# Turning the softmax numerators of the odd heads by DMA instead of on TensorE, in a decoder trunk on one core

## The chip, the core and the metric

One NeuronCore of a Trainium2 chip. Its engines are called PE (TensorE, matrix products), ACT (ScalarE), DVE (VectorE), POOL (GpSimd) and SP (SyncE, which here only issues DMAs). The metric is the device time of one execution in microseconds, lower is better; the time of a kernel is the median of its runs.

## The reference

Two layers over 512 tokens of width 1024, all in float32: a gated short convolution with an MLP, then sparse attention with an MLP, with RMS norms around them. The change is in the attention. There are 16 heads of 64 in 4 groups; the four heads of a group share keys and values. Cut to what matters:

```python
def one_block(qb):                                   # 128 queries
    ...
    logit_c = einsum('bqghd,bngd->bqghn', qt, k_cmp) + bias_c      # 31 compressed blocks
    p_c = softmax(where(valid_c, logit_c, NEG_INF)) * has_any
    o_c = einsum('bqghn,bngd->bqghd', p_c, v_cmp)
    ...
    logit_s = einsum('bqghd,bqgkd->bqghk', qt, ks) + bias_s        # selected blocks
    o_s = einsum('bqghk,bqgkd->bqghd', softmax(where(valid_s, logit_s, NEG_INF)), vs)
    logit_w = einsum('bqghd,bkgd->bqghk', qt, kw) + bias_w[None]   # window of 512
    o_w = einsum('bqghk,bkgd->bqghd', softmax(where(valid_w, logit_w, NEG_INF)), vw)
    return gt[..., 0:1] * o_c + gt[..., 1:2] * o_s + gt[..., 2:3] * o_w
```

The bias is a learned table over 32 buckets of distance, one column per head. With 512 tokens there are 8 blocks to select from and all of them are chosen, so the selected branch and the window branch are both full causal attention, with keys and values of their own.

## The kernel before

**Numbers.** Products are made in fp16 with each operand split into a high and a low half: ACT writes the high half (a scaled copy), DVE the rest (`scaled value - high half`). A product then takes three matmuls (`mm3`: high x high, high x low, low x high). Weights arrive as float32 in pieces, are split by `convert_piece` (L189, L190) and used.

**The attention stage.** Work is cut into items. `Full(g, qb, br, h)` is one head `h` of group `g`, one block `qb` of 128 queries, one branch `br` (selected or window), over `nk = 128 (qb + 1)` keys, that is `nb = qb + 1` blocks of 128. There are 128 of them, 32 per group. `Cmp(g, qb)` is the compressed branch of a group's four heads, 16 items. The order is `full(0) + full(1) + cmps(0) + cmps(1) + full(2) + cmps(2) + cmps(3) + full(3)`. Each item goes through stages at fixed distances behind the front of the list (`lead`):

- `st0`: two products of the queries with the high and the low half of the keys (L878, L879) into a bank "b"; one DVE operation (L883) adds the bias and takes the extreme of each row, from PSUM into a tile `at_s`; ACT takes the exponential and its sum (L886) into `at_p`, float32, one row per query.
- `st1`, two items later: the numerators must stand with the keys on the partitions before they can be multiplied with the values. PE transposes `at_p` block by block in fp32 (L892) into a bank "c"; ACT writes the high half `at_ph` from there (L895).
- `st2`, three items later: DVE writes the low half `at_pl` (L898).
- `st3`, four items later: three products with the values for each block (L910 to L912), into a bank "d" that collects both branches and four heads; after the last head DVE applies the gates and denominators (L921) and POOL adds up.
- `st4`, six items later: `finish` transposes the sum and splits it for the output projection.

Between the stages of the items, a generator `background` puts pieces of projections, 1.7 per item for the first 64 items and 0.9 after: raw keys of the compressed branch (`raw`), the MLP that compresses them (`phi`), the queries of groups 1 to 3 (`queries`), the first half of the output projection. The tile framework places the semaphores and, where an engine's next instruction would wait, may let a later one of the text go first, so the order on an engine is close to the text and not the same.

**The bias.** The row of biases of a head by distance lies in DRAM (`ext_d`). `load_T(g)` reads it as a Hankel matrix, row p shifted by p, for the four heads of a group in one DMA of ACT's queue (L585) into a tile `T` of 128 x 4 x 528 float32, two of them; a small copy `Tc` (L589) holds every 16th column for the compressed branch.

**Shared tiles.** `at_s` (three buffers of 128 x 512 float32) is also taken by `scaled` (L607), whose result ACT and POOL split into queries (L702, L703), and by `raw`, which writes the re-ordered raw keys there (L721) and splits them into `kr_hl` (one buffer, L351, L353); six DMAs on SP then copy that into `big` (L727 to L729). `phi_hd` (L776) is a tile of `phi` that is used once.

Of the kernel before, what the change touches and what calls it, by code (L numbers as in the profile page):

```python
# [29 lines left out]
SP = 1024.0  # L30
# [18 lines left out]
def body(ctx, tc, x, rel_bias, norm_mix, norm_mlp, mlp_w1, mlp_w2, a_w_in, a_conv_w, a_w_out,  # L49
# [512 lines left out]
    with pool("attn") as ap:  # L562
# [17 lines left out]
            DVE.memset(hmask[32 * h:32 * h + 32, h:h + 1], SV / (SR * SW))  # L580
        ot = None

        def load_T(g):
            t = ap.tile([128, 4, TW], F32, name="T", bufs=2)
            nc.scalar.dma_start(t, bass.AP(tensor=ext_d.tensor, offset=ext_d.offset + 4 * g * EXT,  # L585
                                           ap=[[1, 128], [EXT, 4], [1, TW]]))
            TG[g] = t
            c = ap.tile([128, 4, 32], F32, name="Tc", bufs=4)
            DVE.tensor_copy(c, t[:, :, 0:512:16])  # L589
            TC[g] = c  # L590

        load_T(0)
        rbk = rbq = rtok = None
# [9 lines left out]
            DVE.tensor_scalar(rtok[:, 1], r, 1.0 / (SW * SX), None, op0=OP.mult)  # L603

        def scaled(ps, rb):
            t = ftile("at_s", 3)
            DVE.tensor_tensor(t, ps, rb, op=OP.mult)  # L607
            return t

# [100 lines left out]
        def raw(which):  # L710
            po = yield from gated_pair(xkv)
            kr = ap.tile([128, 2, 8, S], F16, name="big", bufs=1)
            DVE.memset(kr[:, :, 4], 0.0)
            DVE.memset(kr[64:128, :, 0:4, S - 1:S], 0.0)
            for half in range(2):
                at = slice(half, S, 64)
                split_to(kr[:, 0, 4, at], kr[:, 1, 4, at], pet[:, which, 8 * half:8 * half + 8], SK)
            for m in range(2):
                t = ftile("at_s", 3)
                by_stride = lambda a: a.rearrange("p (b r) -> p r b", r=16)  # L720
                DVE.tensor_tensor(t.rearrange("p (r b) -> p r b", r=16), by_stride(po[m]), by_stride(rbk),  # L721
                                  op=OP.mult)
                hl = ap.tile([128, 2, S], F16, name="kr_hl", bufs=1)
                split_to(hl[:, 0], hl[:, 1], t)
                for s in range(2):
                    g, r = 2 * m + s, slice(64 * s, 64 * s + 64)
                    nc.sync.dma_start(kr[0:64, :, g, :], hl[r])  # L727
                    nc.sync.dma_start(kr[64:128, :, g, 0:S - 32], hl[r, :, 32:S])
                    nc.sync.dma_start(kr[64:128, :, g, S - 32:S - 1], hl[r, :, 1:32])  # L729
                yield  # L730
            KRs[which] = kr
# [3 lines left out]
        def phi(which):  # L735
            kr = KRs[which]
            ph = [bank("a"), bank("a")]
            for quarter in range(4):
                w = next_piece()
                cv = ahead_fine()  # L740
                for c in range(4):
                    cc = 4 * quarter + c
                    at = 64 * (cc % 8) + cc // 8
                    rhs = [kr[:, hl, 0:5, at:at + 31] for hl in range(2)]
                    for m in range(2):
                        o = ph[m][:, 0:155].rearrange("p (g j) -> p g j", g=5)
                        mm3(o, [u[:, c, m * 128:(m + 1) * 128] for u in w], rhs, cc == 0, cc == 15)
                        next(cv, None)
                    yield
                drain(cv)  # L750
            hs = ap.tile([128, 2, 2, G, 32], F16, name="phi_h", bufs=1)
            DVE.memset(hs[:, :, :, :, 31:32], 0.0)
            for m in range(2):
                bcol = ap.tile([128, 1], F32, name="phi_b", bufs=2)
                ACT.activation(bcol, ph[m][:, 124:125], AF.Copy, scale=1.0 / (SW * SK))
                t = ap.tile([128, G, 31], F32, name="phi_t", bufs=2)
                ACT.activation(t, ph[m][:, 0:124].rearrange("p (g j) -> p g j", g=4), AF.Silu,
                               bias=bcol, scale=1.0 / (SW * SK))
                split_to(hs[:, m, 0, :, 0:31], hs[:, m, 1, :, 0:31], t, SR)
            for _ in range(4):  # L760
                yield
            w = next_piece()
            if which == 0:
                pk = bank("e")
                w2 = [ap.tile([128, 2, 2, 64], F16, name=f"phi_w2{i}") for i in range(2)]
                for i in range(2):
                    for d in range(2):
                        DVE.tensor_copy(w2[i][:, :, d], w[i])
                for m in range(2):
                    mm3(pk[:, 0:128], [u[:, m].rearrange("p a b -> p (a b)") for u in w2],  # L770
                        [hs[:, m, i].rearrange("p g j -> p (g j)") for i in range(2)], m == 0, m == 1)
                split_to(KC[:, 0], KC[:, 1], pk[:, 0:128].rearrange("p (g j) -> p g j", g=4), SK / (SR * SW))
                yield
            else:
                pv = bank("e")
                hd = ap.tile([128, 2, 2, G, 4, 32], F16, name="phi_hd")  # L776
                for m in range(2):
                    for i in range(2):
                        DVE.tensor_copy(hd[:, m, i], hs[:, m, i][:, :, None, :].to_broadcast([128, G, 4, 32]))
                for g in range(4):  # L780
                    o = pv[:, g * 64:(g + 1) * 64]
                    for m in range(2):
                        lh = [hd[:, m, i, g].rearrange("p h n -> p (h n)") for i in range(2)]
                        PE.matmul(o, lh[0], w[0][:, m], start=m == 0, stop=False)
                        PE.matmul(o, lh[0], w[1][:, m], start=False, stop=False)
                        PE.matmul(o, lh[1], w[0][:, m], start=False, stop=m == 1)
                for g in range(4):
                    t = ap.tile([128, 4, 64], F32, name="vc_t", bufs=1)
                    DVE.tensor_tensor(t, pv[:, None, g * 64:(g + 1) * 64].to_broadcast([128, 4, 64]),
                                      hmask[:, :, None].to_broadcast([128, 4, 64]), op=OP.mult)  # L790
                    split_to(VC[:, 0, g], VC[:, 1, g], t)
                yield
            drain(ahead())
# [68 lines left out]
        class Full(Item):  # L862
            def __init__(self, g, qb, br, h):
                self.g, self.qb, self.br, self.h = g, qb, br, h
                self.nb = qb + 1
                self.nk = 128 * self.nb

            def need(self):
                return [f"q{self.g}"]

            def st0(self):
                g, qb, br, h, nk = self.g, self.qb, self.br, self.h, self.nk
                if (g, qb) not in obank:
# [3 lines left out]
                q = Qs[g][:, h, qb * 128:(qb + 1) * 128]  # L877
                PE.matmul(s[:, :nk], q, KD[:, br, 0, g, :nk], start=True, stop=False)  # L878
                PE.matmul(s[:, :nk], q, KD[:, br, 1, g, :nk], start=False, stop=True)  # L879
                lg = ftile("at_s", 3)  # L880
                mn = ap.tile([128, 1], F32, name="at_m", bufs=3)
                lo = 128 * qb + PAD
                DVE.tensor_tensor_reduce(lg[:, :nk], s[:, :nk], TG[g][:, h, lo:lo - nk:-1], -1.0 / SL, 3e38,  # L883
                                         OP.add, OP.min, mn)
                self.p = ftile("at_p", 3)
                ACT.activation(self.p[:, :nk], lg[:, :nk], AF.Exp, bias=mn, scale=-1.0,  # L886
                               accum_out=l[:, br * 4 + h:br * 4 + h + 1])

            def st1(self):
                pt = bank("c")  # L890
                for b in range(self.nb):
                    PE.transpose(pt[:, b * 128:(b + 1) * 128], self.p[:, b * 128:(b + 1) * 128], ident)  # L892
                self.pt = [ap.tile([128, S], F16, name=n, bufs=3) for n in ("at_ph", "at_pl")]
                self.ps = pt[:, :self.nk]
                ACT.activation(self.pt[0][:, :self.nk], self.ps, AF.Copy, scale=SP)  # L895

            def st2(self):
                DVE.scalar_tensor_tensor(self.pt[1][:, :self.nk], self.ps, SP, self.pt[0][:, :self.nk],  # L898
                                         op0=OP.mult, op1=OP.subtract)

# [126 lines left out]
                if next(bg, "end") in ("wait", "end"):  # L1027
                    return

        lead = {1: 2, 2: 3, 3: 4, 4: 6}  # L1030
        credit = 0.0
        for i in range(len(items) + 6):
            if i < len(items):
                it = items[i]
                for k in it.need():
                    while k not in done:
                        if next(bg, "end") == "end":
                            raise RuntimeError(k)
                if isinstance(it, Full):
                    if it.g not in TG:  # L1040
                        load_T(it.g)
                    if (it.qb, it.br, it.h) == (2, 0, 0) and it.g < 3 and it.g + 1 not in TG:
                        load_T(it.g + 1)
                elif it.g not in TC:
                    load_T(it.g)
                it.st0()
            credit += 1.7 if i < 64 else 0.9
            while credit >= 1.0:
# [126 lines left out]
```

## Time and profile before

| | |
|---|---|
| median of 3 runs | 1161.62 us (1160.56 to 1163.6) |
| the profiled execution | 1161.23 us, span 1159.4 us |
| mean granted TensorE clock | 0.990 |
| PE busy | 1109.1 us, 96% |
| DVE busy | 839.8 us, 72% |
| ACT busy | 579.0 us, 50% |
| POOL busy | 146.9 us, 13% |
| attention stage | about 562 to 797 us of the span |

The span runs from the first to the last instruction; the execution's own time has 1.8 us more around it. Busy times count the work of an engine, not its waits. Matmuls are pipelined, so that the busy time of PE, the length of each matmul is more than PE would need at its peak rate. A line such as L330 belongs to the helper `mm3` and has many callers; the tile names tell them apart.

### The profile page before, as it was taken

Reading aid. Unit: us, or ns where it says so; the run is one execution under the profiler, and the core shown is the slowest. Engines: PE = TensorE matmul, PEld = TensorE weight load, DVE = VectorE, ACT = ScalarE, POOL = GpSimd, SP = SyncE. Lnnn points to the kernel's source line nnn. Section 1 sums busy time; section 2 is a strip of 40 time slices with the busy share of each in tenths; the row PEclk is TensorE's granted clock in tenths of the full one; section 3 lists DMA queues with packets and bytes.
Section 4 is the critical chain, followed back from the end, with each engine's and each line's share of the span. In section 5 each row is a group of like instructions: output and inputs, shape, how many; then the busy total and the mean of one; then the engine's idle time right before and its main releaser. Section 6 shows DMA issues by size and latency. Waiting matters only on the chain.

```text
span 1159.4 us, 20318 instructions
## 1 busy us (share of the span) xinstructions
PE 1109.1 (96%) x7947; PEld 694.8 (60%) x7947; DVE 839.8 (72%) x1613; ACT 579.0 (50%) x965; POOL 146.9 (13%) x195
## 2 busy tenths in 40 slices
PE   8999999999999999999899899999999999999886
PEld 3444444447884458858466665665444787446775
DVE  5655458765897557997587898996995698654884
ACT  6322235345343444457579778675544434343442
POOL 0000000422000220000120033111122100123000
PEclk9999999999999999999999999999999999999988
DMA  6432335433433333224233431111733333330321
GB/s 191 126 108 92 109 106 171 121 94 92 128 103 110 98 109 110 92 66 129 89 94 105 119 94 37 38 38 37 212 98 109 110 110 110 109 91 1 94 70 73
DMA packets 147892, 115.76 MB, mean 100 GB/s; under 512 B 8645, under 2 KB 144037, under 8 KB 147797
## 3 DMA queue, kind: packets, MB, share of 16 engines
q1 hardware_dynamic: 145216, 109.47, 31.1%
q10 hardware_dynamic: 2420, 4.48, 1.3%
q8 instruction: 62, 1.02, 0.4%
q0 software_dynamic: 160, 0.52, 0.1%
q14 instruction: 34, 0.27, 0.1%
HBM read 110.22 MB, written 2.14 MB: 97 GB/s over the span
## 4 chain that ended last, share of the span: by engine, by line
PE 51%; DVE 19%; ACT 10%; issue 7%; POOL 6%; DMA 4%; SPq 1%; DVEq 0%; ACTq 0%; POOLq 0%
POOL ml_z L465 6%; PE a L330 5%; PE a L331 5%; PE a L332 4%; DMA wst<-mlp_w_dram 4%; DVE wlo L179 4%; PE b L330 3%; PE b L331 3%; ACT rh L466 3%; PE b L332 3%; PE c L331 3%; PE c L332 3%; PE c L330 3%; DVE wlo L190 3%; DVE wst L176 2%
## 5 line engine op out<-in xcount | busy, mean ns | idle before, releaser
L189 ACT ACTIVATE whi<-wst 128x1024 f16<-128x1024 f32 (+3 forms) x169 | 141.7, 864 | 131.9 <-PE b L331 39.7
L190 DVE SCALAR_TENSOR_TENSOR wlo<-wst,whi 128x1024 f16<-128x1024 f32 (+3 forms) x169 | 167.9, 1001 | 42.1 <-ACT whi L189 42.1
L465 POOL TENSOR_TENSOR ml_z<-ml_z 128x256 f32<-128x256 f32 x128 | 101.1, 810 | 611.2 <-ACT ml_z L463 405.7
L178 ACT ACTIVATE whi<-wst 128x1792 f16<-128x1792 f32 x64 | 106.8, 1691 | 131.4 <-DVE wst L176 93.5
L332 PEld LDWEIGHTS <-wlo 128*128 128x128 f16 x1024 | 100.6, 98 | 109.2 <-issue 2.1
L330 PEld LDWEIGHTS <-whi 128*128 128x128 f16 x1024 | 100.9, 99 | 108.4 <-issue 1.8
L331 PEld LDWEIGHTS <-whi 128*128 128x128 f16 x1024 | 100.6, 98 | 106.7 <-issue 3.8
L467 DVE TENSOR_TENSOR rl<-ml_z,rh 128x1792 f16<-128x1792 f32 x32 | 64.8, 2025 | 135.8 <-ACT rh L466 135.8
L179 DVE SCALAR_TENSOR_TENSOR wlo<-wst,whi 128x1792 f16<-128x1792 f32 x64 | 128.8, 2018 | 6.3 <-ACT whi L178 5.9
L176 DVE TENSOR_TENSOR wst<-wst 128x256 f32<-128x256 f32 x256 | 104.7, 451 | 22.5 <-DMA wst<-mlp_w_dram 21.5
L466 ACT ACTIVATE rh<-ml_z 128x1792 f16<-128x1792 f32 x32 | 54.3, 1697 | 103.3 <-POOL ml_z L465 103.3
L512 PEld LDWEIGHTS <-whi 128*128 128x128 f16 x896 | 88.0, 98 | 18.7 <-ACT ml_t L1087 7.2
L514 PEld LDWEIGHTS <-wlo 128*128 128x128 f16 x896 | 88.0, 98 | 16.7 <-issue 5.0
L513 PEld LDWEIGHTS <-whi 128*128 128x128 f16 x896 | 88.1, 98 | 11.6 <-issue 0.6
L463 ACT ACTIVATE ml_z<-ml_t 128x1024 f32<-128x1024 f32 x32 | 33.8, 1057 | 93.9 <-DVE ml_t L461 93.9
L332 PE MATMUL b<-xsh,wlo 128*128 128x512 f16 x208 | 78.8, 379 | 0.0
L331 PE MATMUL b<-xsl,whi 128*128 128x512 f16 x208 | 78.8, 379 | 0.0
L330 PE MATMUL b<-xsh,whi 128*128 128x512 f16 x208 | 78.7, 379 | 0.0
L886 ACT ACTIVATE at_p<-at_s,at_m 128x128 f32<-128x128 f32 (+3 forms) x128 | 71.3, 557 | 13.7 <-DVE at_m L883 13.3
L512 PE MATMUL a<-rh,whi 128*128 128x256 f16 x256 | 70.5, 275 | 7.0 <-DVE xsh L1089 7.0
L513 PE MATMUL a<-rl,whi 128*128 128x256 f16 x256 | 70.5, 275 | 4.5 <-DVE rl L467 4.5
L883 DVE CUSTOM_DVE_ANT_0 at_s<-b,T 128x128 f32<-128x128 f32 (+3 forms) x128 | 60.9, 479 | 17.0 <-PE b L879 6.6
(292 smaller groups left out, 2761.1 us busy)
## 6 DMA issues: line engine op xcount, KB each, us to landing
wst<-mlp_w_dram SPq DMA_DIRECT2D x256, 256.0 KB, 3.3
wst<-a_w_in_dram SPq DMA_DIRECT2D x24, 512.0 KB, 3.7
wst<-w_kv_dram SPq DMA_DIRECT2D x12, 512.0 KB, 3.5
T<-ext_d ACTq DMA_DIRECT2D x4, 1056.0 KB, 6.6
wst<-a_w_out_dram SPq DMA_DIRECT2D x8, 512.0 KB, 3.4
wst<-b_w_qg_dram SPq DMA_DIRECT2D x8, 512.0 KB, 4.2
wst<-b_w_o_dram SPq DMA_DIRECT2D x8, 512.0 KB, 3.3
xt<-x_dram SPq DMA_DIRECT2D x8, 256.0 KB, 3.7
```

The lines of the kernel that those rows point to most:

```text
L176: DVE.tensor_tensor(b[:, :, o], b[:, :, x], b[:, :, y], op=e)
L178: ACT.activation(hi, b[:, :, 1:], AF.Copy, scale=sc)
L179: DVE.scalar_tensor_tensor(lo, b[:, :, 1:], sc, hi, op0=OP.mult, op1=OP.subtract)
L189: ACT.activation(hi[:, s:e], w, AF.Copy, scale=sc)
L190: DVE.scalar_tensor_tensor(lo[:, s:e], w, sc, hi[:, s:e], op0=OP.mult, op1=OP.subtract)
L330: PE.matmul(ps, w[0], xs[0], start=start, stop=False)
L331: PE.matmul(ps, w[0], xs[1], start=False, stop=False)
L332: PE.matmul(ps, w[1], xs[0], start=False, stop=stop)
L465: POOL.tensor_tensor(z[:, o], z[:, a], z[:, b], op=e)
L466: ACT.activation(rh[0][:, p], z[:, 1:8], AF.Copy)
L512: PE.matmul(acc7[i], wh, xh, start=c == 0 and not other, stop=False, skip_group_check=other)
L513: PE.matmul(acc7[i], wh, xl, start=False, stop=False, skip_group_check=other)
```

## The change

`Full` items with odd `h` are *turned*: `st1` splits `at_p` where it lies, in SBUF, into a tile `at_hl` of 128 x 2nk fp16 (high half, then low half), and one DMA transpose on SP's queue turns all 2nb blocks of 128 x 128 into `at_t`, from which the value products read. Such an item has no `st2`. Even items go through PE as before. For all items the value products come six items behind the front and not four, `finish` eight and not six. Room in SBUF is made: `at_s` has two buffers and not three, `at_ph` and `at_pl` two and not three, the Hankel tiles are held by head (six tiles of one head, loaded one by one, for two tiles of four heads), and `phi_hd` takes the buffer of `kr_hl`, which becomes 128 x 4 x 512.

```diff
-        def load_T(g):
-            t = ap.tile([128, 4, TW], F32, name="T", bufs=2)
-            nc.scalar.dma_start(t, bass.AP(tensor=ext_d.tensor, offset=ext_d.offset + 4 * g * EXT,
-                                           ap=[[1, 128], [EXT, 4], [1, TW]]))
-            TG[g] = t
-            c = ap.tile([128, 4, 32], F32, name="Tc", bufs=4)
-            DVE.tensor_copy(c, t[:, :, 0:512:16])
-            TC[g] = c
+        def load_T(g, heads=range(4)):
+            if g not in TC:
+                TC[g] = ap.tile([128, 4, 32], F32, name="Tc", bufs=4)
+            for h in heads:
+                t = ap.tile([128, TW], F32, name="T", bufs=6)
+                nc.scalar.dma_start(t, bass.AP(tensor=ext_d.tensor, offset=ext_d.offset + (4 * g + h) * EXT,
+                                               ap=[[1, 128], [1, TW]]))
+                TG[g, h] = t
+                DVE.tensor_copy(TC[g][:, h], t[:, 0:512:16])
...
         def scaled(ps, rb):
-            t = ftile("at_s", 3)
+            t = ftile("at_s", 2)
...
-                hl = ap.tile([128, 2, S], F16, name="kr_hl", bufs=1)
+                hl = ap.tile([128, 4, S], F16, name="kr_hl", bufs=1)[:, 0:2]
...
-                hd = ap.tile([128, 2, 2, G, 4, 32], F16, name="phi_hd")
+                hd = ap.tile([128, 4, S], F16, name="kr_hl", bufs=1).rearrange(
+                    "p (m i) (g h n) -> p m i g h n", m=2, g=G, h=4)
...
+                self.turned = h % 2 == 1
...
+            def turn(self):
+                nk, nb = self.nk, self.nb
+                hl = ap.tile([128, 2 * S], F16, name="at_hl", bufs=2)
+                split_to(hl[:, :nk], hl[:, nk:2 * nk], self.p[:, :nk], SP)
+                pt = ap.tile([128, 8, 128], F16, name="at_t", bufs=3)[:, :2 * nb]
+                nc.sync.dma_start_transpose(pt, hl[:, :2 * nk])
+                self.pt = (pt[:, :nb].rearrange("p b q -> p (b q)"), pt[:, nb:].rearrange("p b q -> p (b q)"))
+
             def st1(self):
+                if self.turned:
+                    return self.turn()
...
-                self.pt = [ap.tile([128, S], F16, name=n, bufs=3) for n in ("at_ph", "at_pl")]
+                self.pt = [ap.tile([128, S], F16, name=n, bufs=2) for n in ("at_ph", "at_pl")]
...
             def st2(self):
+                if self.turned:
+                    return
...
-        lead = {1: 2, 2: 3, 3: 4, 4: 6}
+        lead = {1: 2, 2: 3, 3: 6, 4: 8}
...
-                    if it.g not in TG:
-                        load_T(it.g)
-                    if (it.qb, it.br, it.h) == (2, 0, 0) and it.g < 3 and it.g + 1 not in TG:
-                        load_T(it.g + 1)
-                elif it.g not in TC:
-                    load_T(it.g)
+                    if it.g < 3 and (it.qb, it.br, it.h) == (2, 0, 0):
+                        load_T(it.g + 1, (0, 1))
+                    if it.g < 3 and (it.qb, it.br) == (3, 1) and it.h >= 2:
+                        load_T(it.g + 1, (it.h,))
```

More of the change, by code (lines that the diff above doesn't have):

```diff
@@ L718, in raw @@
             for m in range(2):
-                t = ftile("at_s", 3)
+                t = ftile("at_s", 2)
                 by_stride = lambda a: a.rearrange("p (b r) -> p r b", r=16)
@@ L879, in st0 @@
                 PE.matmul(s[:, :nk], q, KD[:, br, 1, g, :nk], start=False, stop=True)
-                lg = ftile("at_s", 3)
+                lg = ftile("at_s", 2)
                 mn = ap.tile([128, 1], F32, name="at_m", bufs=3)
                 lo = 128 * qb + PAD
-                DVE.tensor_tensor_reduce(lg[:, :nk], s[:, :nk], TG[g][:, h, lo:lo - nk:-1], -1.0 / SL, 3e38,
+                DVE.tensor_tensor_reduce(lg[:, :nk], s[:, :nk], TG[g, h][:, lo:lo - nk:-1], -1.0 / SL, 3e38,
                                          OP.add, OP.min, mn)
@@ L1028, in run_bg @@
                     return
-        lead = {1: 2, 2: 3, 3: 4, 4: 6}
+        lead = {1: 2, 2: 3, 3: 6, 4: 8}
         credit = 0.0
-        for i in range(len(items) + 6):
+        for i in range(len(items) + 8):
             if i < len(items):
```

## The prediction

> **What bounds the kernel now.** I read the page first, for the span, then cut the attention stage (first to last work of the `Full` and `Cmp` items, 562 to 797 us; the change touches hardly anything outside it) into stretches, asked for the chain that ended last inside it, and then for its waits.
>
> ```profile
> span 1159.4 us, 20318 instructions
> 562.00:680.00 118.00, 108.71 (x1141) 73.79 (x1140) 93.07 (x280) 94.00 (x256) 13.45 (x14) 0.99 0.35 97
> 680.00:797.00 117.00, 110.63 (x1191) 74.69 (x1189) 108.68 (x391) 86.59 (x263) 27.48 (x40) 1.00 0.15 46
> sum 235.00, PE 219.34 PEld 148.49 DVE 201.76 ACT 180.59 POOL 40.94; mean PE 109.67 PEld 74.24 DVE 100.88 ACT 90.30 POOL 20.47
> ...
> 720.00:780.00 60.00, 58.21 (x641) 40.40 (x641) 58.08 (x208) 43.44 (x135) 8.45 (x14) 1.00 0.15 46
> by line: PE c L892 11.3%; PE a L331 8.9%; PE a L330 8.8%; PE a L332 8.8%; ACT at_p L886 4.7%; PE b L878 4.1%; issue 4.0%; PE b L879 3.9%; PE d L910 3.3%; DVE at_pl L898 3.2%; POOL Q L703 3.1%; DVE at_s L883 2.8%; ACT at_ph L895 2.6%; PE d L
> ```
>
> The columns of the stretches are length, then busy time of PE, weight loads, DVE, ACT and POOL, clock, DMA share, GB/s. In the first half (groups 0 and 1, with much projection work beside them) PE is busy for 108.7 of 118 us and DVE only for 93.1. In the second half DVE is at 108.7 of 117, and from 720 to 780 at 58.1 of 60, 97%. So there are two bounds in turn: PE first, then both with DVE the harder one. On the chain of this stage the largest line is L892, the fp32 transposes of the numerators: 11.3% of 235 us is 26.6 us. That is the work which the change halves.
>
> **What is removed.** A turned item (h odd, 64 of 128) no longer transposes on PE.
>
> ```profile
> L892 PE MATMUL c<-ident,at_p 128*128 128x128 f32 x320 | 57.6, 280 | 6.2 <-DVE at_pl L898 5.5
> L892 PEld LDWEIGHTS c<-ident,at_p 128*128 128x128 f32 x320 | 37.9, 141 | 27.0 <-DVE at_pl L898 9.9 <-issue 4.5 <-ACT at_p L886 2.7
> ```
>
> A group has 2 branches x 4 heads x (1+2+3+4) = 80 blocks; four groups make the 320, and the odd heads own 160. Back to back a transpose follows the one before it at the pace of its fp32 weight load, 141 ns, not at the 280 ns of its busy row, so PE gets 160 x 0.141 = 22.6 us back. How much of that is on the path? Half of L892's share of the chain: 13.3 us. That is the gain I take. Its bounds: 22.6 us if everything that PE gives up is saved, which needs DVE to go from 201.8 to about 212 of 235 without a gap, and nothing if DVE's own queue sets the pace everywhere, as it nearly does between 720 and 780. The turned items also need no bank "c", for which L892 waited on L898 (9.9 us on the weight-load side); this could add a few us and I count it only into the low end of the range.
>
> **What the split costs in its new place.** The two halves of the split stay, one on ACT and one on DVE, but read SBUF.
>
> ```profile
> L895 ACT ACTIVATE at_ph<-c 128x512 f16<-128x512 f32 x32 | 18.7, 586 | 5.6 <-PE c L892 5.6
> L189 ACT ACTIVATE whi<-wst 128x512 f16<-128x512 f32 x41 | 24.7, 623 | 2.7 <-PE a L331 2.7
> L898 DVE SCALAR_TENSOR_TENSOR at_pl<-c,at_ph 128x512 f16<-128x512 f32 x32 | 21.8, 685 | 1.8 <-ACT at_ph L895 1.5
> L190 DVE SCALAR_TENSOR_TENSOR wlo<-wst,whi 128x512 f16<-128x512 f32 x41 | 29.2, 721 | 2.8 <-ACT whi L189 2.8
> ```
>
> L189 and L190 are the same pair of operations from SBUF: 37 ns more on ACT and 36 ns more on DVE. Times 64 that is 2.4 and 2.3 us at the most, into engines that stood idle 54 us (ACT) and 33 us (DVE) in the stage. I take nothing; where DVE is full, the second half, up to 1.2 us would show.
>
> **The DMA transposes.** Each turned item issues one on SP: 128 x 2nk fp16, 64 KB times nb, so 64 to 256 KB, 10.5 MB in all. No transpose by DMA is in this trace. The nearest rows are the copies from SBUF to SBUF of the keys, on the same queue, and above them the loads:
>
> ```profile
> big<-kr_hl SPq DMA_DIRECT2D x8, 128.0 KB, 2.4
> big<-kr_hl SPq DMA_DIRECT2D x8, 7.8 KB, 1.9
> wst<-mlp_w_dram SPq DMA_DIRECT2D x256, 256.0 KB, 3.3
> T<-ext_d ACTq DMA_DIRECT2D x4, 1056.0 KB, 6.6
> L727 SPq DMA_DIRECT2D big<-kr_hl x8: 590/614/702, 580.3 to 648.8; - x8
> ```
>
> Bounds of the landing: 1.9 us (the smallest copy) and 6.6 us (the largest load). I take 2.4 to 3.3 us, by the rows of like size. What it may take: the item is split at two items' distance and its value products are now six behind, four items for split plus landing. The stage is 235 us for 144 items, 1.63 us each; four make 6.5 us. Split, 0.62 + 0.72, and landing, 3.3, make 4.7 us: hidden, with 1.8 us to spare, and the two buffers at_hl (one per two items, so 6.5 us for each) carry it too. Were it late, L910 would stand at the head of PE's queue with the next projections and scores behind it. SP pays some 0.6 us for an issue, 38 us for 64, of 235, beside issues of weights that are as cheap. Weights wait behind a transpose that waits for its DVE half; they are staged pieces ahead, so I take nothing.
>
> On speed the Trainium skill speaks with two voices. "Advanced Engine Details and Errata", X-Bar Transpose (TRN2), has transposing DMAs as fast as ordinary ones; by that the sum above stands. "VectorE: DVE Perf Modes", The three transpose paths, gives 1309 ns for one 128x128 block by DMA against 390 ns on TensorE; 320 blocks one after another would then be an estimated 419 us in a stage of 235. No run before the change shows either.
>
> **What the room for it costs.** SBUF is found by holding less.
>
> *at_s 3 to 2.* This tile takes the logits, the scaled queries and the strided raw keys.
>
> ```profile
> L702 ACT ACTIVATE Q<-at_s x16: 612/627/630, 559.6 to 715.5; 64x512 f16<-64x512 f32 x16
> L703 POOL TENSOR_TENSOR Q<-at_s,Q x16: 1147/1153/1492, 560.3 to 717.4; 64x512 f16<-64x512 f32 x16
> L721 DVE TENSOR_TENSOR at_s<-a,rb x4: 1006/1019/1020, 577.5 to 639.1; 128x512 f32<-128x512 f32 x4
> L351 ACT ACTIVATE kr_hl<-at_s x4: 616/630/631, 578.6 to 645.5; 128x512 f16<-128x512 f32 x4
> DVE at_s L883 <- POOL Q L703: 6.3, 4, 1.8
> DVE at_s L883 <- ACT at_p L886: 3.9, 2, 2.8
> DVE at_pl L898 <- ACT at_ph L895: 7.6, 15, 1.3
> ```
>
> A projection of queries holds two tiles at once, each for two ACT halves and two POOL halves of 1.15 us. With three tiles the logits of DVE already waited there 6.3 us in 4 waits, up to 1.8 us. With two, both can be held, and L883, with all of DVE's later work behind it, waits until the first is free. q1 and q3 fall among `Full` items (q2 among the compressed ones, which don't use at_s): one more longest wait each, 2 x 1.8 = 3.6 us. The second raw tile is written from 639.1 on and read by ACT only at 645.5, after the DMAs of the first; one tile is left for logits meanwhile. I take half the longest wait of DVE on ACT, 0.65 us, for each of two: 1.3 us. Bounds of the whole: nothing if DVE has other work then, 15 us if each of those six tiles costs a 2.5 us stand.
>
> *The keys' DMAs.* L727 to L729 issue six copies of 0.6 us for each raw tile on SP, and one raw phase lies on the chain. Two transposes falling between them, at 0.6 us, make 1.2 us.
>
> *at_ph, at_pl 3 to 2.* Only even items use them now, but an item lives four items, and at its allocation the tile from four items before is still to be read by value products that are next on PE. ACT's high half waits for these, at most 12 products; ACT has the slack (180.6 of 235 us busy), so nothing, and at the worst some 0.3 us x 64 = 19 us. The compressed items keep their buffer counts at the longer distance, so their products come as early as before: nothing.
>
> *Tables by head.* 16 loads of 264 KB in place of 4 of 1056 KB. 12 more issues on ACT, whose row has 366 to 391 ns each, are 4.4 us in ACT's idle 54; the 12 more small copies on DVE, at about 0.2 us, 2 us in its idle 33. Heads 2 and 3 are fetched four items before use, some 6 us: the same cover as above, on the ACT queue. Nothing, and 2 us if DVE has no gap.
>
> ```profile
> L585 ACTq DMA_DIRECT2D T<-ext_d x4: 366/369/391, 507.2 to 678.2; - x4
> L954 DVE TENSOR_TENSOR c_s<-b,Tc x16: 176/218/280, 679.2 to 749.1; 128x32 f32<-128x32 f32 x4, 128x64 f32<-128x64 f32 x4, 128x96 f32<-128x96 f32 x4, 128x128 f32<-128x128 f32 x4
> L886 ACT ACTIVATE at_p<-at_s,at_m x128: 386/570/724, 563.4 to 791.7; 128x128 f32<-128x128 f32 x32, 128x256 f32<-128x256 f32 x32, 128x384 f32<-128x384 f32 x32, 128x512 f32<-128x512 f32 x32
> L910 PE MATMUL d<-VT,at_ph x320: 189/193/203, 569.1 to 796.0; 128*128 128x64 f16 x160
> ```
>
> *The end.* The last item is a turned one. Its exponential ends at 791.7 + 0.7 = 792.4 and its last products came at 796.1, 3.7 us later. Now it is 0.62 + 0.72 + 3.3 + about 0.3 for the products, 4.9 us: 1.2 us more before `finish` and the last output projection.
>
> **The sum.** -13.3 (PE) + 3.6 + 1.3 (at_s) + 1.2 (SP) + 1.2 (end) = -6.0 us. The profiled execution took 1161.23 us (span 1159.4 and 1.8 around it), 0.4 under the median of the three runs, so 1155.2, or 1155.6 on the scale of the median: I say 1155.5.
>
> **Rivals.** *DVE keeps the pace.* PE is relieved, but L883 and L898, which don't shrink, and the stalls on at_s eat the gain. For it: 97% of DVE between 720 and 780. Against it: 25 us of idle DVE before 680. If only the first half's transposes count, half of 13.3, 6.6 us, less the 7.3 us of costs: about 1162, no change.
>
> *Slots in place of PE, slower.* The place is at_s together with at_ph: ACT stands for products, the exponentials come late, and with two tiles the next logits can't start, so DVE stands too. It decides once an item's exponential ends over 1.7 us late (two items, 3.26 us, less the 1.5 us of logits and exponential). At 15 us on at_s and a third of the 19 us on at_ph, against 13.3 of gain and with the other 2.4: 1161 + 15 + 6 + 2 - 13 = 1171.
>
> *A slow turn, slower.* It decides when split and landing pass 6.5 us, a landing of 5.2: then the two at_hl buffers set the pace. At 6.6 us a pair of items takes (1.4 + 6.6) / 2 = 4.0 us in place of 3.26, and 64 pairs add 47 us; the longer half of them only, 24: about 1180 to 1205. Against it: 2.4 us for 128 KB. The serial case of the page on DVE is the far end of this, with 2 in 100 of its own: by rows, 6.6 us for each of the 64 in a row without overlap, 422 us, 190 us more than the stage, 1350.
>
> **Chances.** The forecast case 0.44 (1146 to 1158), no change 0.14, slots 0.28, slow turn 0.12, serial 0.02. I call over 0.3%, 3.5 us, faster or slower; less can't be told from no change. Range 1144 to 1181: below it lies what PE could give beyond half the chain, with 5 in 100; above it most of the slow turns.
>
> **What would show it.** Right: L892 x160; 64 transposes on SP that land in under 4 us; the stretch 562 to 680 shorter by some 6 us or more and DVE's share there up from 79%; L910 hardly waiting on DMA. Wrong: long waits of L910 or of ACT's split on the DMA; waits of L883 on L703 or L886 well above 6.3 and 3.9 us; waits of ACT L895 on products; DVE's total no nearer to the stage's length.

## The result and the profile after

Slower: 1174.88 us median (1169.31 to 1175.58) against 1161.09 (1160.32 to 1163.6) for the kernel before, ratio 1.0118, 95% interval 1.0096 to 1.014; on 1161 us that is 13.7 us. The prediction said 1155.5. The profiled execution took 1175.58 us, its span and the same stretches, groups and waits as before read now (stretches: length, then busy time of PE, weight loads, DVE, ACT and POOL, clock, DMA share, GB/s):

```profile
span 1173.8 us, 20125 instructions
```

```profile
562.00:680.00 118.00, 102.41 (x1019) 67.29 (x1019) 92.58 (x281) 92.10 (x252) 12.66 (x13) 0.93 0.64 138
680.00:797.00 117.00, 99.81 (x1012) 62.32 (x1010) 100.53 (x368) 81.62 (x246) 27.22 (x38) 0.94 0.36 79
720.00:780.00 60.00, 51.51 (x504) 31.95 (x502) 51.62 (x181) 39.47 (x117) 11.06 (x14) 0.94 0.37 85
```

In the first half PE has become idle (108.7 to 102.4 us busy) and no other engine has filled up: DVE 92.6 for 93.1. From 720 to 780 both leaders have fallen, DVE from 58.1 to 51.6, PE from 58.2 to 51.5. So nothing is full any more: the stage waits. The clock is at 0.93 and 0.94 for 0.99 and 1.00, and the DMA share has about doubled. The chain that ended last says for what, in its first entry and its longest pieces (start, length, what). It is asked here from 555 to 830 us, 275 us in all, since the stage now ends later:

```profile
by line: DMA at_t<-at_hl 18.0%; issue 7.8%; PE a L330 5.6%; PE a L331 5.4%; PE a L332 4.8%; ACT at_p L890 4.6%; POOL Q L705 3.7%; PE b L882 2.7%; PE c L906 2.6%; PE b L883 2.6%; PE d L926 2.2%; DVE at_s L887 2.1%; ACT at_hl L351 2.1%; ACT Q
...
609.02 8.07 DMA at_t<-at_hl
...
680.36 5.45 DMA at_t<-at_hl
709.46 4.44 DMA at_t<-at_hl
740.54 6.78 DMA at_t<-at_hl
```

The landing of the transposes leads it with 18.0%, 49.5 us, and the transposes on PE (then L892, now L906) are 7.2 us of it where they were 26.6. The groups of the stage (busy time, mean ns of one, idle before and what ended it), the tile `at_t` (ns to issue, shortest, median and longest) and the waits (total, times, longest):

```profile
L906 PE MATMUL c<-ident,at_p 128*128 128x128 f32 x160 | 31.4, 292 | 2.7 <-ACT at_p L890 2.5
...
L355 DVE SCALAR_TENSOR_TENSOR at_hl<-at_p,at_hl 128x512 f16<-128x512 f32 x16 | 11.5, 718 | 0.4 <-ACT at_hl L351 0.3
...
L351 ACT ACTIVATE at_hl<-at_p 128x512 f16<-128x512 f32 x16 | 10.0, 628 | 4.5 <-DMA at_t<-at_hl 4.3
```

```profile
L898 SPq DMA_TRANSPOSE at_t<-at_hl x64: 1167/1212/2035, 567.2 to 806.8; - x64
...
DMA to landing us min/median/max: 2.3/3.1/8.1
```

```profile
PEld L926 <- DMA at_t<-at_hl: 17.5, 19, 2.4
...
ACT at_hl L351 <- DMA at_t<-at_hl: 13.2, 16, 2.9
...
PE d L926 <- DMA at_t<-at_hl: 11.9, 11, 2.0
...
DVE at_s L887 <- POOL Q L705: 7.3, 4, 2.3
...
DVE Tc L592 <- DMA T<-ext_d: 6.8, 7, 2.0
```

The median landing, 3.1 us, lies in what the prediction took, 2.4 to 3.3; the longest, 8.1, does not. (The trace gives the landing of 49 of the 64.) PE's value products waited 17.5 us for landings, by the row of their weight loads; the 11.9 us of the matmul row lie within the same time and do not add to it. ACT's split waited 13.2 us for its buffer, DVE's small copies 6.8 us for tables. The start of the k-th exponential dates the loss: k=64, the middle, comes at 694.8 us (694.7 before), the last at 803.3 (791.7). The first half was 3.7 us ahead at k=32 and had lost that by its end; the second lost 11.6 us. The rest of the loss, 2.7 us, lies behind the last exponential.

### The profile page after: what moved, and what is told of

It reads as the page before. It is cut to its first block, busy times and chain, and to the rows that moved or that the text cites. A ratio compares the mean times of both kernels' runs of the same rounds, so it can differ in the third digit from the quotient of the medians.

```text
span 1173.8 us, 20125 instructions
## 1 busy us (share of the span) xinstructions
PE 1101.7 (94%) x7787; PEld 682.6 (58%) x7787; DVE 844.1 (72%) x1625; ACT 581.4 (50%) x963; POOL 148.9 (13%) x195
## 4 chain that ended last, share of the span: by engine, by line
PE 31%; DVE 24%; ACT 13%; DMA 12%; issue 10%; POOL 9%; SPq 0%; DVEq 0%; ACTq 0%; POOLq 0%
POOL ml_z L465 7%; DMA wst<-mlp_w_dram 6%; DVE wlo L179 6%; DMA at_t<-at_hl 4%; ACT rh L466 4%; DVE wst L176 4%; PE a L330 3%; PE a L331 3%; DVE wlo L190 3%; PE a L332 3%; DVE ml_t L461 3%; ACT ml_z L463 3%; PE b L331 2%; PE b L330 2%; PE b L332 2%
## 5 line engine op out<-in xcount | busy, mean ns | idle before, releaser
L331 PEld LDWEIGHTS <-whi 128*128 128x128 f16 x1024 | 100.7, 98 | 108.7 <-issue 4.5
L513 PEld LDWEIGHTS <-whi 128*128 128x128 f16 x896 | 88.1, 98 | 11.6 <-issue 0.6
L463 ACT ACTIVATE ml_z<-ml_t 128x1024 f32<-128x1024 f32 x32 | 33.9, 1058 | 92.6 <-DVE ml_t L461 92.6
```

Of the source, the lines that this page charges most:

```text
L331: PE.matmul(ps, w[0], xs[1], start=False, stop=False)
L513: PE.matmul(acc7[i], wh, xl, start=False, stop=False, skip_group_check=other)
```

## The experiments

Each time stands beside the kernel before, run on the same chip in the same comparison.

**Is PE's relief worth anything?** `relief` is the kernel before with PE's work taken away and no DMA: odd items are split in SBUF and read unturned, which is not the reference's product. `at_ph` and `at_pl` have two buffers and `phi_hd` lies in the buffer of `kr_hl`, as in the change.

```diff
+                if self.turned:
+                    hl = ap.tile([128, 2 * S], F16, name="at_hl", bufs=2)
+                    split_to(hl[:, :nk], hl[:, nk:2 * nk], self.p[:, :nk], SP)
+                    self.pt = (hl[:, :nk], hl[:, nk:2 * nk])
```

> The kernel before, with its distances, its three at_s and its tables, in which the odd items split in SBUF into at_hl and the value products read these unturned halves (not the reference's product): PE is relieved of 160 transposes and nothing else changes but two buffers for at_ph, at_pl. If the relief is worth what I put (13.3): 1148. If DVE takes the pace as soon as PE is relieved: 1155 to 1160.

Measured 1156.28 us, ratio 0.9969 (0.9958 to 0.9981), the range of DVE taking the pace. From 720 to 780 its DVE is busy 57.97 of 60 us: there the relief brings nothing. The first half was 7.4 us ahead at k=32 and had lost that by k=64 (694.3 us). Where it was lost, the clock had fallen; the kernel before, and `relief` below it:

```profile
635.00:640.00 5.00, 2.80 (x29) 1.90 (x27) 4.26 (x10) 3.77 (x11) 1.11 (x1) 1.00 0.68 223
640.00:645.00 5.00, 3.32 (x40) 2.22 (x40) 4.94 (x18) 2.84 (x12) 0.00 (x0) 1.00 0.53 111
```

```profile
630.00:635.00 5.00, 2.54 (x32) 1.66 (x30) 5.00 (x13) 4.31 (x14) 1.10 (x1) 0.90 0.55 157
635.00:640.00 5.00, 3.96 (x26) 2.43 (x26) 3.39 (x12) 2.52 (x9) 0.00 (x0) 0.50 1.04 267
640.00:645.00 5.00, 3.41 (x21) 1.98 (x20) 2.85 (x10) 1.97 (x6) 0.00 (x0) 0.58 0.49 113
```

```profile
PE d L922 <- DVE o_t L933: 1.8, 1, 1.8
```

The last three columns are clock, DMA share and GB/s. In `relief` PE stood 1.8 us at 631.5 for a tile of DVE's (the last line; DVE was full, 5.00 of 5), was busy for 2.54 of 5 us, and the granted clock went to 0.50. `relief_warm` puts work there that nobody reads:

```diff
+                wd = bank("e")
+                for k in range(24):
+                    PE.matmul(wd, xkv[0][:, k % 8, 0:128], xkv[0][:, k % 8], start=True, stop=True)
```

> This kernel is relief (distances, buffers and tables of before; the odd items' numerators split in SBUF and read by the value products unturned, 1156.3 us) with 24 spare fp16 matmuls of 128x512 into bank e, whose result nobody reads, put behind the keys' copies of the second raw phase, where relief's granted clock fell to 0.50 (635 to 640 us) and 0.58 (640 to 645). Theory 'clock': PE's gap there lowers the clock, and with the gap filled the clock stays at 1.0 from 630 to 655, the item at k=64 (694.3 us in relief) starts some 5 us earlier or more in spite of the 24 x 0.22 us, and the time is about 1150 to 1154. Rival 'the first half is bound by something else, and the low clock costs nothing': k=64 as late as in relief or later, time 1156 to 1162.

1149.73 us, ratio 0.9891 (0.9874 to 0.9909), a little better than the clock theory asked, and the exponential k=64 comes at 686.6 us, 7.7 earlier than in `relief`. The clock stayed up where `relief` had lost it and dipped once behind that, after a gap of 2.4 us:

```profile
635.00:640.00 5.00, 4.64 (x46) 2.72 (x43) 4.92 (x16) 5.00 (x16) 0.00 (x0) 1.00 0.61 144
640.00:645.00 5.00, 2.53 (x12) 1.38 (x11) 4.91 (x14) 3.67 (x12) 0.60 (x1) 0.85 0.59 138
```

The control, the same spare work in the kernel before:

> A control for relief_warm: the kernel before with the same 24 spare matmuls in the second raw phase, nothing else. Theory 'clock': before keeps a clock of 1.00 at that place (3.4 us of clock lost in its whole stage, the sum of 1 less the granted clock), so there is nothing to win: 1160 to 1166, the 24 x 0.22 us in part on the path. Rival 'the spare matmuls help by the order that they give to the other work': some 5 us faster than before as relief_warm was than relief, 1153 to 1157.

1162.82 us, ratio 1.001 (0.9994 to 1.0025): nothing won where the clock was full. So the spare work is not good by itself. That `relief` lost to its clock is supported by both. Not all of the 0.0078 (9 us) between `relief` and `relief_warm` is shown to be clock: the sum of (1 - clock) over the stage is 8.5 us in `relief` and 3.4 in `relief_warm` and before, a difference of 5.

`after_keepPE` is the change with PE's transposes of the odd items put back, into a bank that nobody reads:

```diff
+                pd = bank("c")
+                for b in range(nb):
+                    PE.transpose(pd[:, b * 128:(b + 1) * 128], self.p[:, b * 128:(b + 1) * 128], ident)
```

> The change with PE's work put back: odd items go the way by DMA as in the change, and PE also transposes their numerators into bank c, which nobody reads. Theory 'PE is not what the change waits for': about as the change, 1172 to 1178, perhaps less since PE's gaps are filled and the clock (0.979 in the change) stays up. Rival 'the relief of PE is worth what the prediction took, 13 us': 1183 to 1190.

1184.64 us, ratio 1.0196 (1.0174 to 1.0217), 0.0078 or 9 us over the change, in the range of the rival. My theory that PE is not what the change waits for fell: putting the transposes back costs some 9 us. That taking them away is worth as much is not shown by it, and the next kernels say otherwise.

**What do the transposes cost?** Three kernels take the change apart: `no_turn` (`self.turned = False`, room for it: `at_ph`, `at_pl` 5), `free_turn` (no DMA, the products read `at_hl` unturned, five of them) and `unread` (the DMAs run, the odd products read a tile of keys in place of `at_t`).

```diff
-                self.pt = (pt[:, :nb].rearrange("p b q -> p (b q)"), pt[:, nb:].rearrange("p b q -> p (b q)"))
+                self.pt = (KD[:, self.br, 0, self.g, :nk], KD[:, self.br, 1, self.g, :nk])
```

> The change without its transposes by DMA: every item goes through PE, at_ph and at_pl have five buffers so that products six items behind can wait; at_s with two buffers, tables by head and the new distances stay. Theory L (the transposes land late: PE stands, and its clock sinks): about the time of before, 1158 to 1165, with no DMA wait of the value products. Theory S (the room made for them, at_s above all, and the longer distance cost the time): 1168 or more.

> The change with the split in SBUF but no DMA: the value products of the odd items read the unturned halves from at_hl (five buffers), which is not the reference's product. PE, ACT and DVE do the same work as in the change. Theory L: the relief of PE shows, 1145 to 1155. Theory S: still 1165 or more, since at_s and the distances are as in the change.

> The change with all its DMA transposes, but the value products of the odd items read a tile of keys instead of the turned numerators (not the reference's product), so PE never waits for a landing; ACT's split still waits for a free at_hl, and the queue and the DMA engines carry the same load. Theory L with PE's wait as its main part: 1150 to 1160, near free_turn. If the wait of ACT for at_hl or the load on the queue is the main part: 1168 to 1175, near the change. Theory S: near the change too.

`no_turn`: 1162.9 us, ratio 1.002 (1.0004 to 1.0037), as theory L said. `free_turn`: 1162.14 us, 1.0006 (0.9992 to 1.0019), which neither theory gave. `unread`: 1169.71 us, 1.0077 (1.0047 to 1.0108), in the range of ACT's wait or the queue's load, not of PE's wait. As a chain from the kernel before to the change: the room and the longer distance cost 0.0020 (2.3 us); PE's relief then wins 0.0014 (1.6 us, not told apart from nothing); running the DMAs, with two buffers of `at_hl` for the five of `free_turn`, costs 0.0071 (8.2 us); and PE's waiting for them costs 0.0041 (4.8 us). The last two are uncertain by some 4 us each.

**The room.** `before_ats2` is the kernel before with `ftile("at_s", 2)`.

> The kernel before with two buffers of at_s in place of three and nothing else. Theory S: 1165 to 1172. Theory L: within 3 us of before; my priced term was 4.9 us.

1165.62 us, ratio 1.0043 (1.0031 to 1.0056): 5.0 us for the 4.9 priced, as theory S said. But `no_turn`, which has this, the tables by head and the longer distance, costs 2.3 us in all: such costs, measured one by one, do not add up.

**The tables.** `after_T0` uses group 0's tables for all groups; `after_T0_s3_hl3` fills the room that this frees with a third `at_s` and a third `at_hl`; `T0_s3_hl3_unread` has PE wait for no landing besides, by the edit of `unread`.

```diff
+        for g in range(1, 4):
+            TC[g] = TC[0]
+            for h in range(4):
+                TG[g, h] = TG[0, h]
```

> The change, but the tables of group 0 serve all groups (a wrong bias for the others): 12 of the 16 table loads and their small copies in the stage are gone. Theory T (the tables by head come late and DVE stands for them, and their DMAs hold up the transposes): 1165 to 1168. If only the landings beside weights and the buffers count: 1172 to 1175.

> As after_T0, with the room of the two freed tables given to a third at_s and a third at_hl. Theory of slots (ACT waits for at_hl until the DMA has read it, logits wait for at_s): 1155 to 1160, with ACT's wait for the DMA gone. If the load on queue and engines costs the time: within 4 us of after_T0 less the 4.8 us that at_s cost by itself.

> after_T0_s3_hl3 (1161.2 us: the change without its later tables, with at_s 3 and at_hl 3; PE still waits 27 us for landings) where the odd items' products read a tile of the keys and so wait for no landing; the transposes are issued as before. Theory 'PE's waits for the landings hide the relief, which is worth some 10 us': 1150 to 1155. Rival 'the DMAs cost by what they keep busy (SP, the engines beside the weights), not by PE's waits': 1158 to 1162.

`after_T0`: 1167.1 us, ratio 1.0062 (1.0043 to 1.0081), as theory T said. `after_T0_s3_hl3`: 1161.19 us, 1.0007 (0.999 to 1.0023), just over the range of the slots: the two buffers win 6.4 us, of which at_s by itself was 5.0, although ACT's wait for `at_hl` fell from 14.3 us to 3.6. `T0_s3_hl3_unread`: 1155.96 us, 0.9958 (0.9939 to 0.9977), between theory and rival. Who waited for the tile `at_t` in the second and, below it, in the third of them, with the issues and landings:

```profile
  PEld L930: 17.0, 20
  PE d L930: 10.0, 15
  ACT at_hl L351: 3.6, 3
```

```profile
L902 SPq DMA_TRANSPOSE at_t<-at_hl x64: 1167/1215/3680, 567.9 to 790.6; - x64
...
  ACT at_hl L351: 3.1, 3
...
DMA to landing us min/median/max: 2.3/3.1/5.6
```

That gives the loss in steps of another order, in ratios times 1161: with all 64 transposes running, unread, with three buffers each and no later tables, the kernel is 4.9 us faster than before. From there PE's waits for landings lose 5.7 us, the two missing buffers 6.4, the later tables 6.5: 13.7 over the kernel before. (Each step is uncertain by some 3 us.) The first of these kernels is as fast as `relief`, which has no DMA, so no cost of SP's 1.2 us per transpose and of the traffic can be seen. A few us are not ruled out: `relief` had lost to its clock, and the same kernel without its DMAs was not run. Most of the 8 us of `unread` would then go with the two buffers and the late tables.

Are the tables traffic or waiting? `after_T0_traffic` puts the 12 loads back into tiles that nobody reads, without the copies; `before_tables` is the kernel before with the tables by head alone.

```diff
+                        td = ap.tile([128, TW], F32, name="Td", bufs=2)
+                        nc.scalar.dma_start(td, bass.AP(tensor=ext_d.tensor, offset=ext_d.offset + (4 * it.g + 4 + h) * EXT,
+                                                        ap=[[1, 128], [1, TW]]))
```

> after_T0 (the change with the tables of group 0 used for all groups, so a wrong bias for groups 1 to 3; 1167.1 us) with the 12 later table loads put back into tiles that nobody reads, and without their small copies on DVE. It tells apart what the tables by head cost. Theory 'traffic': the 3.2 MB beside the transposes slow their landing: 1172 to 1175, about as the change. Theory 'waiting': the loads are harmless by themselves, and it was DVE that waited for a late table or for its small copy: 1166 to 1169.

> The kernel before with the tables held by head, loaded at the places of the change, and nothing else. Leaving these loads and copies out of the change won 7.8 us (after_T0). Theory 'they cost only beside the transposes': 1160 to 1163. Rival 'they cost by themselves, late tables and copies on DVE': 1165 to 1169.

`after_T0_traffic`: 1169.44 us, ratio 1.0064 (1.0049 to 1.0079): as `after_T0`, so it is not the traffic but the copies and the waits for the tables. Nor did the loads delay the transposes: the longest landing is 5.7 us with them and 5.5 without. `before_tables`: 1164.41 us, ratio 1.0028 (1.0017 to 1.004): 3.3 us with no transpose in the kernel, between the two ranges expected. Its tile `T`, and its small copies: the last load is issued at 739.0 us and its copy runs at 742.9, where in the kernel before these were 678.2 and 711.3 and no copy waited for a load:

```profile
L592 DVE COPY Tc<-T x16: 117/180/194, 517.2 to 742.9; 128x32 f32<-128x32 f32 x16
...
  DMA T<-ext_d: 3.6, 5
...
DMA to landing us min/median/max: 3.1/3.9/4.2
```

DVE stood 3.6 us for five tables, about the 3.3 us; that they are the same is argued, not shown. In the change the same wait is 6.8 us and the tables land as late as 7.4 us.

**Can it be mended?** Five kernels tried; none beats the kernel before. `wpool` issues the stage's weights on POOL's queue. `room` has all buffers back (`at_s` 3, a third split tile, `phi_hd` in `big`) and the small copies at their first use. `turn_big` turns query blocks 2 and 3 only; `room_big` is both, with the tables of groups 2 and 3 loaded among the compressed items. `after_warm` puts the 24 spare matmuls, and 8 ahead of each of five late products, into the change.

```diff
-                nc.sync.dma_start(v, src)
+                wq[0].dma_start(v, src)
...
-            t = ftile("at_s", 2)
+            t = ftile("at_s", 3)
...
-                self.turned = h % 2 == 1
+                self.turned = h % 2 == 1 and qb >= 2
...
+                if (g, qb, br, h) in FILL:
+                    wd = bank("e")
+                    for k in range(8):
+                        PE.matmul(wd, VT[:, 0, 0, 0:128], VT[:, 0, 0], start=True, stop=True)
```

> The change, with the weights of the attention stage issued by POOL in place of SP, so that SP has only the transposes and the keys' copies. Theory Q (a transpose lands late because it stands behind 512 KB of weights in its own queue): landings of 2.3 to 3.1 us everywhere but beside the tables, and 1166 to 1170. If the DMA engines themselves are shared, whatever the queue: landings as in the change and 1173 to 1178.

> The change with its room found otherwise, all of the reference computed: at_s back to three buffers (phi_hd in a tile of big, kr_hl back to two halves), a third buffer for the split numerators (every third turned item uses a work tile), and the small copies of a table on DVE put at their first use, not at the load. If at_s (priced 4.9, measured 4.8), ACT's wait for at_hl (14.3 us with two buffers, 3.6 with three) and the small copies are most of the loss of 13.8 us, 1161 to 1166. If the landings of the transposes beside the weights and tables are the loss by themselves, 1168 to 1173.

> The change, but only the odd heads of the query blocks 2 and 3 are turned by DMA (32 items in place of 64, 112 of their 160 blocks); the others go through PE. In the change the items of blocks 0 and 1 come at some 0.85 to 1.2 us each, so that four of them don't hold the split and even an undisturbed landing of 2.3 us, and their products wait (2.3 us of landing, 0.05 us between landing and product, nine items of groups 2 and 3). Theory 'distance': half of the loss of 13.8 us goes, 1165 to 1170. Rival 'only the landings beside loads count' (these are at block 3, but one): 1172 to 1176. Rival 'PE's relief is what is missed': over 1176.

> room (1175.4 us) with the transposes kept away from what disturbed them: only blocks 2 and 3 are turned, the tables of groups 2 and 3 are loaded among the compressed items, where nothing is turned, and heads 0 and 1 of group 1 early in group 0. All of the reference is computed. Theory 'waits for landings and the clock that they lower are what room loses': the gain of relief (3.8 us) comes through in part, 1154 to 1162. Rival 'the split from SBUF and the longer distance cost by themselves': 1163 to 1170. If neither place nor number of the transposes matters: 1172 to 1177.

> The change with spare work where PE stands: the 24 spare matmuls of relief_warm, and 8 spare matmuls (8 x 0.22 us) ahead of the value products of five turned items whose landing PE waited for in the change (before its clock dips at 616, 648, 684, 712 and 745 us). Waits, DMAs and buffers are as in the change, PE gets some 14 us more to do. Theory 'clock' (the change loses 16.0 us of clock in its stage and before 3.4, and the 12.6 us between are most of its loss of 13.8): the dips go in part and the time is 1162 to 1170. Rival 'the waits themselves are the loss': 1174 to 1180.

`wpool`: 1189.0 us, ratio 1.0255 (1.0205 to 1.0305), landings 2.3/3.1/7.7 (shortest, median, longest): weights ahead of the transposes on SP's queue were not the reason. It is slower than both expectations, and why is open. `room`: 1175.36 us, ratio 1.0119 (1.0102 to 1.0135), nothing won, against both theories. Its `at_t`:

```profile
  PEld L935: 31.1, 22
  PE d L935: 24.3, 16
...
DMA to landing us min/median/max: 2.3/3.1/8.8
```

PE waits 31.1 us for landings (the weight loads' row again), for 17.0 in `after_T0_s3_hl3`, which differs by the tables and by the places of the third split tile, of the copies and of `phi_hd`. So the steps above do not add up in any order; with the tables there, ACT's wait for split tiles is down to 2.0 us and PE's has grown. Which of the differences does it stays open. `turn_big`: 1172.87 us, ratio 1.0098 (1.0066 to 1.0129), not told apart from the change: theory *distance* is not borne out. PE's waits for landings fell to 9.7 us, but the small items are PE's again. `room_big`: 1170.51 us, ratio 1.0073 (1.0053 to 1.0093), some 5 us of the 13.7 won, well short of the theory's 1154 to 1162. `after_warm`: 1177.15 us, ratio 1.0125 (1.0099 to 1.0152), in the range of its rival. Here the sum of (1 - clock) over the stage's 5 us stretches fell from 16.0 us to 5.6 (before: 3.4), and nothing was won. The spare work was some 14 us, PE's gaps over 0.7 us stayed at 23 us in all (24 in the change), so it seems to have lain beside the gaps and to have cost what the clock gave. Whether the clock is part of the change's loss is therefore open.

## Why the prediction was wrong, point by point

The forecast was -6.0 us and +13.7 was measured, 19.7 us apart. Two steps failed: the landing that was to be hidden, and the relief of PE that was to reach the time. The chain over `no_turn` puts 11.7 us of the difference on the relief (1.6 for 13.3) and 10.6 on the transposes (13.0 for the 2.4 of SP and the end), and its room cost 2.6 less than priced. The chain over `after_T0` puts 6.0 on the relief with SP and the end, 5.7 on PE's waits, 1.5 on buffers and 6.5 on the tables. How much belongs to which depends on the order, and that stays open.

- **The landing, "hidden, nothing", is the first step that failed.** Its cover was worked out from a mean, 1.63 us an item, so 6.5 us for four. Items come in bursts: in the kernel before the exponentials 72 to 80 start within 6.8 us, 0.85 each, and four make 3.4. Landings of 2.3 and 2.4 us, the shortest there are, then left their product waiting, 0.5 and 0.2 us, in groups 2 and 3. And some landings took 4 to 8 us, among them the one issued at 609.02 between two table loads. The tables are not shown to be the cause: without any later table `after_T0_s3_hl3` has a landing of 7.8 us, and the longest of `unread`, 8.8, has weights beside it and no table. What makes a landing long is open. PE's waiting costs 5 to 6 us.
- **The at_hl buffers** were called enough by the same mean; ACT stood 13.2 us for them. A third one is worth 1.4 us, the 6.4 of both buffers less the 5.0 of at_s, within the noise.
- **at_s**, 4.9 us, measured 5.0 by itself. The wait named for it, L883 on L703, barely grew (6.3 to 7.3). And the term says half the longest wait of DVE on ACT and takes 0.65 us, but the longest in its lines is 2.8, so by its own rule it is 6.4. That the size agrees is in part luck.
- **Tables by head, "nothing"**: 3.3 us alone, and 6.5 in the change as the last step. Cover of the load was asked for; what stands behind the small copy in DVE's queue was not.
- **PE's relief, 13.3 us, is the second step that failed.** `after_keepPE` says 9, `relief` 3.6, `free_turn` against `no_turn` 1.6, and `relief_warm`, with a clock that stayed up, 12.7. So the size can be had, and in the change's own room it was not. In `relief` the clock took part of it, and DVE keeps the pace in the second half, as the rival *DVE keeps the pace* said; in `free_turn`, whose clock is as good as before, where it went is open. The upper bound was also too high: the transposes of the kernel before start 0.109 us apart, not 0.141, so 17.4 us and not 22.6.
- **The end**, 1.2 us: from the last exponential's end to the last product it is 6.5 us for 3.9, so 2.6. `free_turn` has 6.4 without any DMA, so a landing is not needed for it.
- **The split from SBUF**: 628 and 718 ns for 586 and 685, as priced; **at_ph two**: L909 waited for PE's transposes as before (7.3 us, 17.9 then) and 2.0 us for products, as good as priced. **SP**: 1.2 us an issue for 0.6, without an effect that can be seen.
- Of the rivals, *a slow turn* has the mechanism (its signs, L926 and ACT's split waiting on the DMA, are the first waits), but not its price: it took every landing as 6.6 us, 1180 to 1205. The median stayed at 3.1. *Slots* gave nearly the time, 1171, but of its mechanism the runs show only at_s, with 5.0 us for its 15.

## What to carry to other kernels

A latency is hidden by the work that lies beside it at that place, not by the stage's mean: take the shortest pitch of items and the longest landing that the same queues show under load. A copy that waits for a load holds up what is queued behind it: 3.6 us for five tables here, and 0.3 us in `room`, where the copies stand at their first use (`room` won nothing by it). Costs and gains measured one by one in the old kernel need not add up in the new one. And taking work off the leading engine opens gaps; look at the granted clock right behind them before counting the gain.

## What the runs showed of the hardware

A transpose by DMA of 128 rows landed in 2.3 to 2.4 us for one and two blocks of keys (64 and 128 KB) and some 3.05 us for four (256 KB) when little else ran, and held SP 1.17 to 1.24 us in most cases (2.0 at the longest). The Trainium skill gives 1309 ns for one 128x128 block by DMA ("VectorE: DVE Perf Modes", The three transpose paths); eight such blocks in 3.05 us show that it is not paid block by block. "Advanced Engine Details and Errata", X-Bar Transpose (TRN2), has them as fast as ordinary DMAs; the trace agrees where they run alone (256 KB of weights: 3.3 us).

The granted clock changes in pieces of 3.41 us in these traces, so the busy share of such a piece tells more than that of 5 us. The piece ahead of the fall in `relief`, and below it the emptiest one at that place in the kernel before, where the clock stayed at 1.00:

```profile
630.58:634.00 3.42, 1.37 (x20) 0.91 (x19) 3.42 (x9) 3.12 (x9) 0.64 (x1) 1.00 0.55 163
```

```profile
638.95:642.36 3.41, 1.93 (x29) 1.39 (x25) 3.35 (x12) 2.39 (x8) 0.86 (x1) 1.00 0.37 81
```

The first is 40% busy with no gap longer than 1.8 us, the second 57%. From 540 to 830 us of all twenty profiles, all 50 pieces at full clock with PE busy under 45% were followed by half clock, none of the 1498 over 57%, and 18 of the 54 between. Half clock ended only behind pieces that were busy for 82% or more. The Trainium skill, "TensorE: Matmul & The Clock Gate", Part 1, tells of a free-running window of some 3.4 us after which an idle PE gets half its clock; the 0.50 agrees, and the runs show besides that PE needn't be idle throughout for it.
